# A hybrid encoder trunk on one core: a Fourier front whose roots, folds and first squares stand elsewhere

## The chip, the cores and the metric

The kernel runs on one core of a Trainium2 chip. The metric is the device time of one execution in microseconds (us); several executions are timed and their median is given.

## The reference

Two sequences of 512 tokens with 1024 channels, a prompt and a sample, go through two layers. The first mixes tokens by a grouped two-dimensional Fourier transform, the second by attention; each is followed by a squared-ReLU MLP. All arithmetic is float32. The change lies in the first mixer:

```python
def rms_norm(x, g):
    y = x32 * lax.rsqrt(jnp.mean(x32 * x32, axis=-1, keepdims=True) + EPS)
    return (y * g)

def fourier_mix(h, w_out):
    hg = h.reshape(B, S, N_FGROUPS, F_GROUP)          # 8 groups of 128 channels
    f = jnp.fft.fft2(hg, axes=(1, 3), norm="ortho").real
    return f.reshape(B, S, D_MODEL) @ w_out

for i in range(DEPTH):                                # DEPTH = 2
    if i % 2 == 0:
        x = x + fourier_mix(rms_norm(x, fourier_norm[j]), fourier_w_out[j])
    else:
        x = x + gqa_attention(rms_norm(x, attn_norm[j]), ...)
    x = x + sq_relu_mlp(rms_norm(x, mlp_norm[i]), mlp_w_up[i], mlp_w_down[i])
return rms_norm(x, final_norm)
```

## The kernel before

The engines are called by the names of the profile: PE does matrix products, DVE is the vector engine, ACT the scalar engine, POOL is GpSimd, and SP issues most DMAs. A float32 product is made of three products of halves: a value is split into a high half (a rounding copy by ACT, L86) and a low half (the difference, by DVE, L87). Everything that the change touches stands in one block in which the instructions of every engine run in the order in which the code was written; after some 90 us the rest of the two layers follows.

The first 75 us or so of that block, with `q=0` for the prompt and `q=1` for the sample:

- **Front.** `f0` and `f1` each take two of the prompt's four tiles of 128 tokens (`g0` and `g1` those of the sample). `squares` (L430) sums the squares of a tile's rows on ACT, `chain` makes the root of the mean from it (the five steps of `log_steps`: one of ACT's, with a logarithm and an exponential, L141 and L142, and four short ones of DVE, L145 to L149, for both tiles at once), `gain` multiplies by the norm's gain, `plus` and `minus` add and subtract the two halves of 512 channels, `scale` (L461), `scale_both` (L467) and `combine` multiply by the root. While the first inputs land, PE runs filler products (`idle`, L603).
- **The exact transform** (`transform(0)`). Along the tokens, the prompt's transform runs in plain float32, in three parts `k=0, 1, 2` (f0's two tiles, then f1's pair). Each part has, for each block `j` of 128 channels, an even product of 258 columns (`exact_even`, L531) and an odd one of 256 (`exact_odd`, L534), and a small one for the last frequency (`exact_nyq`, L537). Three blocks are accumulated over `k=0, 1`, each even and odd product in a PSUM bank of its own; after `mid()` come the `k=2` products, and the fourth block follows with all its six products after the first feature stage. `seq_evac` copies a block out, `feat_stage` transforms it along the channels (L571, L579, L580), and its result is split into halves `uv`.
- **The weights' folds.** `Fold(j)` holds two 128x1024 parts of `w_four`: DVE subtracts them (L672), and a DMA issued by POOL adds the second part from memory to the first (L673). `odd` splits the difference, `even_hi` and `even_lo` (L682, L686) the sum. `FoldNyq` does the same for the last frequency: three small operations of POOL (L701 to L703), a DMA to memory, and three DMAs back (L706).
- **Products with the folds.** `odd_outs` (L81 to L83) makes eight outputs, `k` outermost, from the halves `uv` and the odd folds; `even_outs` makes them one output at a time from the even folds, with a last product for the last frequency (L724).
- **The sample's transform** (`transform(1)`) runs in halves. Its `hook1` places the prompt's first MLP squares (`square`, L167, ACT) between the copies that PE waits for; POOL adds up the eight squares (L173), the sum is split (L195, L199), and PE's root product (L213) needs it.

Of the kernel before, what the change touches and what calls it, by code (L numbers as in the profile page):

```python
# [19 lines left out]
P = 128  # L20
D = 1024
# [23 lines left out]
def trunk_kernel(ctx, tc, x_in, xt_in, y_out, tables, rope, gfour, gcol, grow, gfin,  # L45
# [375 lines left out]
    class Front:  # L421


        def __init__(self, q, c):
            self.q, self.c = q, c
            self.ss, self.r = small(2), small(2)
            self.steps = log_steps(self.r[:, :2], self.ss[:, :2], 2, 1.0 / D)
            self.xg, self.p, self.m = [None] * 2, [None] * 2, [None] * 2

        def squares(self, i):  # L430
            sumsq(xa[self.q, 2 * self.c + i], self.ss[:, i : i + 1])
# [19 lines left out]

        def chain(self, a, b):
            for step in self.steps[a:b]:
                step()
            if b == 5 and self.c == 0 and self.q:
                self.rm = small(1)
                nc.gpsimd.tensor_mul(self.rm[:, :1], self.r[:, 1:2], mask)
# [12 lines left out]
        def combine(self):  # L470
# [9 lines left out]
            n = sm.tile([P, 2, 64], F32R, tag="ny", name=nm("ny"), bufs=2)  # L480
            nc.gpsimd.memset(f32(n), 0.0)
# [48 lines left out]
    def exact_even(k, j, o):  # L530
        nc.tensor.matmul(o[:, :258], parts[k][0][:, j * P : (j + 1) * P], cosX[k], start=k == 0, stop=k == 2)  # L531

    def exact_odd(k, j, v):
        nc.tensor.matmul(v[:, :256], parts[k][1][:, j * P : (j + 1) * P], sinX[k], start=k == 0, stop=k == 2)  # L534
# [16 lines left out]
    def seq_evac(q, o, v):  # L551
        if q == 0:
            t = slot([P, 514], F32)
            nc.scalar.copy(t[:, :258], o[:, :258])
            nc.scalar.copy(t[:, 258:], v[:, :256])
            return t[:, :258], t[:, 258:]
# [12 lines left out]
    def feat_stage(q, j, a, b, an, en, u=None):  # L569
        if q == 0:  # L570
            nc.tensor.matmul(u[:, :258], ftX[:, :P], a, start=False, stop=True)  # L571
# [6 lines left out]
        if q == 0:  # L578
            nc.tensor.matmul(v[:, :256], ftX[:, P:], b, start=True, stop=True)  # L579
            nc.tensor.matmul(en[0:72, :258], pickX[:, pick], a, start=j == 0, stop=j == 3)  # L580
# [10 lines left out]
    def nyq_out(q, en):  # L591
        t = slot([P, 258], F32R)[0:72]
        nc.scalar.copy(t, en[0:72, :258])
        nc.vector.tensor_sub(t[64:72], en[64:72, :258], f32(t[64:72]))
        un[q] = t
# [9 lines left out]
    def transform(q, mid=lambda: None, hook=lambda at, j: None):  # L605
        on, ov = ps(), [(ps(), ps()) for _ in range(3)]
        if q == 0:
            for k in range(2):
                for j in range(3):
                    exact_even(k, j, ov[j][0])  # L610
                exact_nyq(k, on)
                for j in range(3):
                    exact_odd(k, j, ov[j][1])
            mid()
            exact_nyq(2, on)
        else:
            seq_nyq(q, 0, on)
# [1561 lines left out]
```

## Time and profile before

| what | value |
|---|---|
| median of 3 executions | 1665.58 us (1665.34 to 1665.73) |
| profiled execution, its own time | 1665.18 us |
| span of that execution | 1663.4 us, so 1.78 us lie around the span |
| busy, of the span | DVE 1267.9 us (76%), ACT 882.2 (53%), POOL 383.7 (23%) |
| granted TensorE clock | 9 tenths or more of full speed in each of 40 slices |

The span runs from the first to the last instruction that the profiler recorded. Times in the timeline views are counted from its start.

### The profile page before, as it was taken

How to read it: one execution, taken by the hardware profiler on the slowest of the kernel's cores; microseconds unless marked ns; L12 is line 12 of the kernel's file. 1: busy time of each engine (PE TensorE's matmuls, PEld its weight loads, DVE VectorE, ACT ScalarE, POOL GpSimd, SP SyncE). 2: the span in 40 equal slices, each digit the busy share in tenths (PEclk: the TensorE clock that was granted, in tenths of full speed). 3: DMA queues.
4: the chain of work that ended last, by engine and by line, in shares of the span. 5: the costliest groups of instructions: out<-in, count | busy, mean ns of one | idle time of the engine just before them, and what ended most of it. 6: DMA issues, size and time to landing. Idle time of an engine off the chain costs nothing.

```text
span 1663.4 us, 22119 instructions
## 1 busy us (share of the span) xinstructions
PE 1653.9 (99%) x7768; PEld 1380.1 (83%) x7768; DVE 1267.9 (76%) x1818; ACT 882.2 (53%) x1566; POOL 383.7 (23%) x363
## 2 busy tenths in 40 slices
PE   9999999999999999999999999999999999999998
PEld 8988888888888888888888888888888888888887
DVE  8898786557886869868788878877855487878875
ACT  7776454446343425447688856554554553433335
POOL 3311443222000001324544303004422220000002
PEclk9999999999999999999999999999999999999999
DMA  9843554359775757425401146334544696757532
GB/s 310 255 159 133 191 209 171 140 186 373 239 234 167 242 181 231 171 72 196 171 1 39 64 172 231 129 108 178 202 147 169 222 375 194 232 161 231 180 108 102
DMA packets 122336, 302.48 MB, mean 182 GB/s; under 512 B 12360, under 2 KB 13768, under 8 KB 122224
## 3 DMA queue, kind: packets, MB, share of 16 engines
q1 hardware_dynamic: 98864, 253.66, 43.4%
q0 software_dynamic: 8960, 21.05, 5.9%
q10 hardware_dynamic: 14400, 26.35, 4.2%
q8 instruction: 61, 1.00, 0.2%
q14 instruction: 51, 0.42, 0.1%
HBM read 217.59 MB, written 82.38 MB: 180 GB/s over the span
## 4 chain that ended last, share of the span: by engine, by line
PE 98%; DVE 1%; issue 0%; DMA 0%; ACT 0%; POOL 0%; POOLq 0%; DVEq 0%; SPq 0%
PE ps L983 76%; PE ps L83 6%; PE ps L81 6%; PE ps L82 6%; PE ps L1586 2%; PE ps L1565 0%; DMA u<-x 0%; DVE u L437 0%; PE ps L213 0%; PE ps L534 0%; PE ps L531 0%; DVE u L1928 0%; POOL t L1580 0%; DVE t L450 0%; DVE t L441 0%
## 5 line engine op out<-in xcount | busy, mean ns | idle before, releaser
L983 PE MATMUL ps<-u,w 128*128 128x512 f32 x4944 | 1129.9, 389 | 0.0
L983 PEld LDWEIGHTS ps<-u,w 128*128 128x128 f32 x4944 | 927.1, 188 | 195.1 <-ACT u L1018 2.4
L86 ACT CAST w<-raw 128x1024 fp32r<-128x1024 f32 (+1 forms) x216 | 213.4, 994 | 312.3 <-PE ps L983 232.4
L87 DVE TENSOR_TENSOR w<-raw,w 128x1024 fp32r<-128x1024 f32 (+1 forms) x216 | 250.5, 1164 | 63.4 <-ACT w L86 59.5
L86 ACT CAST u<-u 128x1024 fp32r<-128x1024 f32 x144 | 144.8, 1048 | 87.6 <-PE ps L983 35.2
L87 DVE TENSOR_TENSOR u<-u,u 128x1024 fp32r<-128x1024 f32 x144 | 173.0, 1229 | 20.8 <-ACT u L86 20.2
L983 PE MATMUL ps<-u,u 128*128 128x512 f32 x600 | 142.8, 389 | 0.0
L1202 DVE TENSOR_TENSOR u<-ps,u 128x512 f32<-128x512 f32 x160 | 109.4, 685 | 39.7 <-PE ps L983 37.0
L1103 POOL TENSOR_TENSOR u<-u 128x512 f32<-128x512 f32 x28 | 37.8, 1352 | 428.8 <-ACT u L1000 428.8
L1229 POOL DMA_DIRECT2D raw<-w_sum x32 | 27.7, 865 | 468.3 <-DVE w L87 165.4
L983 PEld LDWEIGHTS ps<-u,u 128*128 128x128 f32 x600 | 112.6, 188 | 23.4
L81 PE MATMUL ps<-u,u 128*128 128x512 f32 (+2 forms) x340 | 128.6, 380 | 0.0
L83 PE MATMUL ps<-u,u 128*128 128x512 f32 (+2 forms) x340 | 123.7, 365 | 0.0
L82 PE MATMUL ps<-u,u 128*128 128x512 f32 (+2 forms) x340 | 123.6, 364 | 0.0
L173 POOL TENSOR_TENSOR t<-t,t 128x512 f32<-128x512 f32 (+1 forms) x49 | 69.3, 1419 | 185.7 <-ACT t L167 184.9
L999 ACT ACTIVATE t<-t 128x512 f32<-128x512 f32 x64 | 40.4, 631 | 111.1 <-DVE t L1072 101.3
L83 PEld LDWEIGHTS ps<-u,u 128*128 128x128 f32 x340 | 64.2, 189 | 10.4 <-DVE u L87 0.3
L87 DVE TENSOR_TENSOR u<-ps,u 128x512 fp32r<-128x512 f32 (+3 forms) x112 | 68.0, 634 | 6.1 <-ACT u L86 5.7
L82 PEld LDWEIGHTS ps<-u,u 128*128 128x128 f32 x340 | 64.4, 189 | 8.5 <-DVE u L87 0.8
L81 PEld LDWEIGHTS ps<-u,u 128*128 128x128 f32 x340 | 64.4, 189 | 7.7
L1059 DVE TENSOR_TENSOR t<-ps,u 128x512 f32<-128x512 f32 x32 | 22.0, 688 | 62.0 <-PE ps L983 51.4
L86 ACT CAST u<-ps 128x512 fp32r<-128x512 f32 (+3 forms) x112 | 59.0, 555 | 7.5 <-PE ps L1586 5.8
(269 smaller groups left out, 2016.3 us busy)
## 6 DMA issues: line engine op xcount, KB each, us to landing
raw<-w_up SPq DMA_DIRECT2D x80, 512.0 KB, 4.5
u<-spill_t SPq DMA_DIRECT2D x60, 512.0 KB, 7.0
raw<-w_sum SPq DMA_DIRECT2D x56, 512.0 KB, 5.4
u<-spill_b SPq DMA_DIRECT2D x45, 512.0 KB, 6.1
spill_t<-u SPq DMA_DIRECT2D x84, 256.0 KB, 2.0
spill_b<-t ACTq DMA_DIRECT2D x60, 256.0 KB, 4.1
raw<-w_row SPq DMA_DIRECT2D x28, 512.0 KB, 4.6
park<-u SPq DMA_DIRECT2D x24, 512.0 KB, 4.3
```

Source lines behind the costliest of these rows:

```text
L81: nc.tensor.matmul(out, lh, rh, start=first, stop=False)
L82: nc.tensor.matmul(out, lh, rl, start=False, stop=False)
L83: nc.tensor.matmul(out, ll, rh, start=False, stop=last)
L86: hi = nc.scalar.copy(dst_hi, src)
L87: return hi, eng.tensor_sub(dst_lo, src, f32(dst_hi))
L173: nc.gpsimd.tensor_add(acc[q][:, :n], acc[q][:, :n], s[:, :n])
L983: nc.tensor.matmul(o, w[x][:, sl], h[k][y], start=first and k + i == 0, stop=k == n - 1 and i == 2, skip_group_check=not first)
L999: nc.scalar.activation(t, src, AF.Relu)
L1103: eng.tensor_sub(t[:, 0], b12, b11)
L1202: return nc.vector.tensor_add(x, o, x)
L1229: nc.gpsimd.dma_start(s[:, 1], w[:, 3], accum_op=ALU.add)
L1586: nc.tensor.transpose(pt[:, t * P : (t + 1) * P], probs[t][:, sc * P : (sc + 1) * P], ident)
```

## The change

- A root is made by POOL, tile by tile, with two operations on 128x1 values (`root`: add eps, raise to the power -1/2), in place of `chain`; ACT's square is scaled so that it sums the mean. There are 22 fillers instead of the second run of 26.
- In the exact transform, the even product (now 257 columns) and the odd one (255) of a block share a PSUM bank, so that four banks hold four blocks: the fourth block's `k=0, 1` products are done with the others. One copy of 128x512 takes a block out.
- For folds 2 and 3, DVE writes the difference to a new buffer and POOL adds on chip (`tensor_add`, 128x1024), instead of the adding DMA. `FoldNyq`'s small operations come after f1's second root, and its DMAs back (`spread`) after fold 1's `minus`. The even halves of folds 2 and 3 are made ahead of those of 0 and 1.
- The first two even outputs are made together, `k` outermost.
- In `transform(1)`, the squares that stood after the first three blocks (`seq`) stand after the third block, the first feature stage, the fourth block, the second stage, and two each after the third and fourth stages.

```diff
         def __init__(self, q, c):
-            self.steps = log_steps(self.r[:, :2], self.ss[:, :2], 2, 1.0 / D)
         def squares(self, i):
-            sumsq(xa[self.q, 2 * self.c + i], self.ss[:, i : i + 1])
+            if self.q and i == 0:
+                self.n = sm.tile([P, 2, 64], F32R, tag="ny", name=nm("ny"), bufs=2)
+                nc.gpsimd.memset(f32(self.n), 0.0)
+            junk = tm((P, 1024), BF16)
+            nc.scalar.activation(junk, xa[self.q, 2 * self.c + i], AF.Square, scale=D ** -0.5,
+                                 accum_out=self.ss[:, i : i + 1])
+        def root(self, i):
+            nc.gpsimd.tensor_tensor(out=self.ss[:, i : i + 1], in0=self.ss[:, i : i + 1], in1=eps, op=ALU.add)
+            nc.gpsimd.tensor_tensor(out=self.r[:, i : i + 1], in0=self.ss[:, i : i + 1], in1=half, op=ALU.pow)
+            if i and self.c == 0 and self.q:
+                self.rm = small(1)
+                nc.gpsimd.tensor_mul(self.rm[:, :1], self.r[:, 1:2], mask)
         def gain(self, i, k=None, o=None):
...
-        def chain(self, a, b):
-            for step in self.steps[a:b]:
-                step()
-            if b == 5 and self.c == 0 and self.q:
-                self.rm = small(1)
-                nc.gpsimd.tensor_mul(self.rm[:, :1], self.r[:, 1:2], mask)
...
     def exact_even(k, j, o):
-        nc.tensor.matmul(o[:, :258], parts[k][0][:, j * P : (j + 1) * P], cosX[k], start=k == 0, stop=k == 2)
-    def exact_odd(k, j, v):
-        nc.tensor.matmul(v[:, :256], parts[k][1][:, j * P : (j + 1) * P], sinX[k], start=k == 0, stop=k == 2)
+        nc.tensor.matmul(o[:, :257], parts[k][0][:, j * P : (j + 1) * P], cosX[k][:, :257], start=k == 0, stop=k == 2)
+    def exact_odd(k, j, o):
+        nc.tensor.matmul(o[:, 257:], parts[k][1][:, j * P : (j + 1) * P], sinX[k][:, 1:], start=False, stop=k == 2,
+                         skip_group_check=True)
     def exact_nyq(k, o):
...
     def seq_evac(q, o, v):
         if q == 0:
-            t = slot([P, 514], F32)
-            nc.scalar.copy(t[:, :258], o[:, :258])
-            nc.scalar.copy(t[:, 258:], v[:, :256])
-            return t[:, :258], t[:, 258:]
+            t = slot([P, 512], F32)
+            nc.scalar.copy(t, o)
+            return t[:, :257], t[:, 257:]
...
     def transform(q, mid=lambda: None, hook=lambda at, j: None):
-        on, ov = ps(), [(ps(), ps()) for _ in range(3)]
+        on = ps()
         if q == 0:
+            ov = [(ps(), None) for _ in range(NT)]
-                for j in range(3):
+                for j in range(NT):
-                for j in range(3):
-                    exact_odd(k, j, ov[j][1])
+                for j in range(NT):
+                    exact_odd(k, j, ov[j][0])
             mid()
+            ov = [(ps(), ps()) for _ in range(3)]
...
-        o3 = ps(), ps()
+        o3 = (ps(), ps()) if q else ov[3]
         if q == 0:
-            for k in range(3):
-                exact_even(k, 3, o3[0])
-            for k in range(3):
-                exact_odd(k, 3, o3[1])
+            exact_odd(2, 3, o3[0])
+            exact_even(2, 3, o3[0])
...
         def minus(self):
-            nc.vector.tensor_sub(self.b, self.a, self.b)
-            nc.gpsimd.dma_start(self.a, w_four[1, self.j], accum_op=ALU.add)
+            if self.j < 2:
+                nc.vector.tensor_sub(self.b, self.a, self.b)
+                nc.gpsimd.dma_start(self.a, w_four[1, self.j], accum_op=ALU.add)
+                return
+            b, self.b = self.b, slot([P, D], F32)
+            nc.vector.tensor_sub(self.b, self.a, b)
+            nc.gpsimd.tensor_add(self.a, self.a, b)
         def odd(self):
...
         def load(self):
+        def fold(self):
+        def spread(self):
...
         wn.load()
-        idle(ps(), 26)
-        f0.squares(0)
-        f0.squares(1)
+        idle(ps(), 22)
+        for i in range(2):
+            f0.squares(i)
+            f0.root(i)
-        f0.chain(1, 2)
+        f0.plus(0)
+        f0.minus(0)
+        f0.scale_both(0)
+        for k in range(2):
+            f0.gain(1, k, halves_gr[k])
+        f0.plus(1)
+        f0.minus(1)
-        f0.minus(0)
-        f0.chain(0, 1)
-        f0.chain(2, 5)
-        f0.plus(0)
-        f0.scale_both(0)
-        f0.gain(1)
-        f0.minus(1)
-        f0.plus(1)
+        f1.root(0)
+        f1.minus(0)
+        f1.plus(0)
-        f1.chain(1, 2)
-        f1.minus(0)
+        f1.root(1)
+        wn.fold()
+        f1.scale()
+        f1.minus(1)
+        f1.plus(1)
         fold = [Fold(j) for j in range(2)]
         def mid():
-            f1.chain(0, 1)
-            f1.plus(0)
-            f1.chain(2, 5)
-            f1.scale()
-            f1.minus(1)
-            f1.plus(1)
...
             if at == "seq":
                 if j == 0:
+                    wn.spread()
                 elif j == 2:
...
             elif j == 3:
-                g0.squares(0)
-                g0.gain(0)
-                g0.minus(0)
-                g0.plus_there(0)
-                g0.squares(1)
-                g0.gain(1)
-                g0.minus(1)
-                g0.plus_there(1)
+                for i in range(2):
+                    g0.squares(i)
+                    g0.root(i)
+                for i in range(2):
+                    fold[2 + i].even_hi()
+                    g0.gain(i)
+                    g0.minus(i)
+                    g0.plus_there(i)
         transform(0, mid, hook0)
-        g0.chain(0, 2)
+        for i in range(2):
+            fold[2 + i].even_lo()
+        g0.scale(slice(0, 1))
+        fold[0].even_lo()
-        g0.chain(2, 5)
-        fold[0].even_lo()
-        g0.scale(slice(0, 1))
-        fold[2].even_hi()
-        fold[2].even_lo()
-        odd_put(0, 0, o[0])
-        fold[3].even_hi()
-        fold[3].even_lo()
-        for fo in range(1, 4):
+        for fo in range(2):
+            odd_put(0, fo, o[fo])
+        for fo in range(2, 4):
...
-        def even(fo):
-            even_put(0, fo, even_outs(0, [fo])[0])
+        def even(fo, o=None):
+            even_put(0, fo, o or even_outs(0, [fo])[0])
         g1.squares(0)
-        even(0)
+        g1.root(0)
+        o = even_outs(0, range(2))
+        even(0, o[0])
         g1.squares(1)
-        even(1)
+        g1.root(1)
+        even(1, o[1])
-        g1.chain(0, 2)
-        g1.chain(2, 5)
...
+        due = iter(range(KC))
         def hook1(at, j):
-            if at == "seq":
-                if j < 3:
-                    square(0, j)
-            else:
-                square(0, 3 + j)
-                if j == 3:
-                    square(0, 7)
+            for _ in range({("seq", 2): 1, ("feat", 0): 1, ("seq", 3): 1, ("feat", 1): 1,
+                            ("feat", 2): 2, ("feat", 3): 2}.get((at, j), 0)):
+                square(0, next(due))
         transform(1, hook=hook1)
```

PE's rows of the exact transform up to the first feature stage (L531 and L534, now L534 and L537, are the even and odd products, the 40-row ones those of the last frequency; the bank stands ahead of the arrow). Before, from the first products of `k=1` on:

```order
L531 MATMUL ps_261<-u_110,t_223 128x258
L537 MATMUL ps_256<-u_110,ny_213 40x258
L534 MATMUL ps_258<-u_116,t_221 128x256
L534 MATMUL ps_260<-u_116,t_221 128x256
L534 MATMUL ps_262<-u_116,t_221 128x256
L537 MATMUL ps_256<-u_116,ny_289 40x258
L534 MATMUL ps_258<-u_116,t_285 128x256
L531 MATMUL ps_257<-u_116,t_278 128x258
```

And of the change:

```order
L534 MATMUL ps_250<-u_110,t_199 128x257
L541 MATMUL ps_246<-u_110,ny_192 40x258
L537 MATMUL ps_247<-u_116,t_201 128x255
L537 MATMUL ps_248<-u_116,t_201 128x255
L537 MATMUL ps_249<-u_116,t_201 128x255
L537 MATMUL ps_250<-u_116,t_201 128x255
L541 MATMUL ps_246<-u_116,ny_269 40x258
L537 MATMUL ps_247<-u_116,t_230 128x255
L534 MATMUL ps_247<-u_116,t_216 128x257
```

Each part now has a fourth block's product (bank ps_250) ahead of the products that wait for f1 (t_230, t_216; before t_285, t_278); four such products come there from the place after the first feature stage.

POOL's rows from its first arithmetic on. Before:

```order
L701 TENSOR_TENSOR u_158<-u_158 128x64
L702 CAST u_158<-u_158 128x64
L703 TENSOR_TENSOR u_158<-u_158 128x64
L704 DMA nyq<-u_158 128x2x64
L706 DMA u_155<-nyq 8x1024 x3
L673 DMA raw_238<-w_four 128x1024
L673 DMA raw_242<-w_four 128x1024
L673 DMA raw_297<-w_four 128x1024
L673 DMA u_301<-w_four 128x1024
```

And of the change, from f1's second root on:

```order
L439 TENSOR_TENSOR s_148<-s_147,half 128x1
L713 TENSOR_TENSOR u_152<-u_152 128x64
L714 CAST u_152<-u_152 128x64
L715 TENSOR_TENSOR u_152<-u_152 128x64
L716 DMA nyq<-u_152 128x2x64
L679 DMA raw_234<-w_four 128x1024
L679 DMA raw_238<-w_four 128x1024
L720 DMA u_149<-nyq 8x1024 x3
L683 TENSOR_TENSOR raw_277<-raw_277,u_278 128x1024
L683 TENSOR_TENSOR u_281<-u_281,u_282 128x1024
```

Four roots (eight rows) stand ahead of `FoldNyq` now, and the two adds of folds 2 and 3 (L683) are queued behind the three DMAs that wait for `nyq`.

ACT's rows in `transform(1)` (L86 copies the halves that PE waits for, L167 are the squares). Before, from the first square on:

```order
L167 ACTIVATE t_832<-u_427 128x512
L86 CAST u_842<-ps_785 128x258
L86 CAST t_843<-ps_786 128x256
L167 ACTIVATE t_848<-u_427 128x512
L86 CAST u_859<-ps_787 128x258
L86 CAST t_860<-ps_788 128x256
L167 ACTIVATE t_865<-u_428 128x512
L86 CAST u_879<-ps_868 128x257
L86 CAST u_879<-ps_873 128x255
L167 ACTIVATE t_884<-u_428 128x512
```

And of the change, the same copies from the second block on:

```order
L86 CAST u_812<-ps_757 128x258
L86 CAST t_813<-ps_758 128x256
L86 CAST u_826<-ps_759 128x258
L86 CAST t_827<-ps_760 128x256
L167 ACTIVATE t_832<-u_415 128x512
L86 CAST u_845<-ps_834 128x257
L86 CAST u_845<-ps_839 128x255
L167 ACTIVATE t_850<-u_415 128x512
```

The first square stands where the third stood, and the second where the fourth stood.

## Rows read from the trace of the kernel before

**Rows 1.** The page: busy time, share of the span and instructions of PE.

```profile
PE 1653.9 (99%) x7768; PEld 1380.1 (83%) x7768; DVE 1267.9 (76%) x1818; ACT 882.2 (53%) x1566; POOL 383.7 (23%) x363
```

**Rows 2.** PE's waits: line, releaser, then total us, times, longest.

```profile
PE ps L537 <- DVE ny L475: 0.4, 1, 0.4
PE ps L531 <- ACT t L467: 0.4, 1, 0.4
...
PE ps L1586 <- POOL t L1580: 0.2, 1, 0.2
```

**Rows 3.** Timeline of PE, 5 to 30 us: start, us, engine, line.

```profile
5.92 3.56 PE L603 MATMUL ps<-u 128*128 128x256 f32 x26
9.84 1.57 PE L531 MATMUL ps<-u,t 128*128 128x258 f32 x6 [0.36 <-ACT t L467]
...
15.26 1.56 PE L534 MATMUL ps<-u,t 128*128 128x256 f32 x6
17.25 0.63 PE L537 MATMUL ps<-u,ny 128*40 128x258 f32 x2 [0.44 <-DVE ny L475]
...
20.55 0.60 PE L531 MATMUL ps<-u,t 128*128 128x258 f32 x2
...
29.64 0.28 PE L81 MATMUL ps<-u,u 128*128 128x256 f32 x1
```

**Rows 4.** Timeline of ACT, 4 to 21 us.

```profile
5.80 0.19 ACT L130 ACTIVATION_READ_ACCUMULATOR t<-u 128x1 f32 x1
...
9.06 0.72 ACT L467 ACTIVATE t<-t,s 128x512 f32<-128x512 f32 x1 [0.26 <-DVE t L441]
...
14.30 0.19 ACT L130 ACTIVATION_READ_ACCUMULATOR t<-u 128x1 f32 x1
```

**Rows 5.** Timeline of DVE, 4 to 42 us.

```profile
6.31 0.69 DVE L437 TENSOR_TENSOR u<-u,ps 128x512 f32<-128x512 f32 x1 [0.17 <-PE ps L382]
...
18.57 1.22 DVE L672 TENSOR_TENSOR u<-raw,u 128x1024 f32<-128x1024 f32 x1
...
26.74 1.22 DVE L87 TENSOR_TENSOR u<-u,u 128x1024 fp32r<-128x1024 f32 x1
27.87 2.07 DVE L87 TENSOR_TENSOR u<-ps,u 128x257 fp32r<-128x257 f32 x6
```

**Rows 6.** Timeline of POOL, 3 to 58 us.

```profile
12.01 0.79 POOL L701 TENSOR_TENSOR u<-u 128x64 f32<-128x64 f32 x1 [9.55 <-DMA u<-w_nyq]
...
13.53 1.18 POOL L703 TENSOR_TENSOR u<-u 128x64 fp32r<-128x64 f32 x1
...
20.84 1.55 POOL L706 DMA_DIRECT2D u<-nyq  x3 [4.85 <-DMA nyq<-u]
```

**Rows 7.** One line of POOL, last in the kernel: duration ns min/median/max, starts.

```profile
L1910 POOL TENSOR_TENSOR s<-s,half x2: 667/812/957, 1654.8 to 1658.6; 128x1 f32<-128x1 f32 x2
```

**Rows 8.** Timeline of POOL and of DVE at 88 us: both read two tiles.

```profile
88.65 1.30 POOL L173 TENSOR_TENSOR t<-t,t 128x512 f32<-128x512 f32 x1 [19.18 <-ACT t L167]
...
89.26 1.78 DVE L278 TENSOR_TENSOR u<-u,u 128x1024 fp32r<-128x1024 f32 x1
```

**Rows 9.** Timelines of ACT, POOL, DVE and PE, 56 to 73 us.

```profile
60.94 0.69 ACT L167 ACTIVATE t<-u 128x512 f32<-128x512 f32 x1
...
59.58 4.03 POOL L173 TENSOR_TENSOR t<-t,t 128x512 f32<-128x512 f32 x3 [1.13 <-ACT t L167]
64.06 5.41 POOL L173 TENSOR_TENSOR t<-t,t 128x512 f32<-128x512 f32 x4 [0.45 <-ACT t L167]
...
70.16 0.69 DVE L199 TENSOR_TENSOR u<-t,u 128x512 fp32r<-128x512 f32 x1 [0.23 <-ACT u L195]
...
71.45 0.63 PE L213 MATMUL ps<-u,minus 128*128 128x512 f32 x2
```

**Rows 10.** Timelines of DVE and PE at 56 us.

```profile
56.12 0.68 DVE L506 TENSOR_TENSOR u<-t,u 128x512 fp32r<-128x512 f32 x1
...
56.85 0.28 PE L83 MATMUL ps<-u,u 128*128 128x258 f32 x1
```

More of the change, by code (lines that the diff above doesn't have):

```diff
@@ L479, in combine @@
                 return
-            n = sm.tile([P, 2, 64], F32R, tag="ny", name=nm("ny"), bufs=2)
-            nc.gpsimd.memset(f32(n), 0.0)
+            n = self.n
             n32 = sm.tile([P, 16], F32, tag="n32", name=nm("n32"), bufs=2)
@@ L570, in feat_stage @@
         if q == 0:
-            nc.tensor.matmul(u[:, :258], ftX[:, :P], a, start=False, stop=True)
+            nc.tensor.matmul(u[:, :257], ftX[:, :P], a, start=False, stop=True)
         else:
@@ L578, in feat_stage @@
         if q == 0:
-            nc.tensor.matmul(v[:, :256], ftX[:, P:], b, start=True, stop=True)
-            nc.tensor.matmul(en[0:72, :258], pickX[:, pick], a, start=j == 0, stop=j == 3)
+            nc.tensor.matmul(v[:, 1:256], ftX[:, P:], b, start=True, stop=True)
+            nc.tensor.matmul(en[0:72, :257], pickX[:, pick], a, start=j == 0, stop=j == 3)
         else:
@@ L591, in nyq_out @@
     def nyq_out(q, en):
-        t = slot([P, 258], F32R)[0:72]
-        nc.scalar.copy(t, en[0:72, :258])
-        nc.vector.tensor_sub(t[64:72], en[64:72, :258], f32(t[64:72]))
+        t, n = slot([P, 258], F32R)[0:72], 258 if q else 257
+        if q == 0:
+            nc.gpsimd.memset(f32(t[:, 257:]), 0.0)
+        nc.scalar.copy(t[:, :n], en[0:72, :n])
+        nc.vector.tensor_sub(t[64:72, :n], en[64:72, :n], f32(t[64:72, :n]))
         un[q] = t
@@ L627, in transform @@
             if q == 0:
-                exact_odd(2, j, ov[j][1])
+                exact_odd(2, j, ov[j][0])
                 exact_even(2, j, ov[j][0])
```

## The prediction

> **What bounds the kernel now.** The page comes first: PE is busy for 1653.9 of 1663.4 us [rows 1], so only PE's idle time, and work taken off PE, can change the time. Second the list of what PE waits for: two of 0.4 us lie in the exact transform, and the only one after the first 80 us is of 0.2, on L1586 [rows 2]. What the change does in those 80 us is therefore handed on unchanged to the end, if no later margin catches it. Third the timelines of the front, engine by engine. The reader should see in PE's that fillers run from 5.92 us, the first exact product starts at 9.84, the products of `k=0, 1` end at about 16.66 (a row of six instructions starts at 15.26 and shows 1.56 us, of which the last 0.17 is the modelled tail), the small product of f1 starts at 17.25, and the last of its row group at 20.55 [rows 3]. Each exact product is two instructions, about 0.433 us.
>
> 0.2% of the time is 3.3 us; that is what a measurement of this kernel can tell from no change.
>
> **The change, part by part.**
>
> *Start of the exact transform: -1.0 us.* The first product waited for ACT's scale of 0.72 us at 9.06, which waited for the root and DVE [rows 4]. Now the square of tile 0 is read out at 5.99 us [rows 4], and the root needs two POOL operations. A power on 128x1 takes 0.67 to 0.96 us [rows 7]; the add I take at 0.5 (below 0.79, which POOL needs for 64 columns [rows 6]). So the root is there at 7.2 to 7.5. DVE's second gain starts at 6.31 and ends at 7.0 [rows 5], the `plus` behind it needs as much, to 7.7, and the scale 0.72, to 8.4. PE's fillers end at 9.48 in the row, of which some 0.16 is modelled tail, so that a product could have followed at 9.32; 26 in 3.56 us are 0.12 to 0.13 each, and four fewer end at 8.84. PE goes on there without a wait: 9.84 - 8.84 = 1.0 us. If both operations took 1.18 us, POOL's longest small one [rows 6], the root came at 8.35, the scale ended at 9.07, and 0.8 were left.
>
> *The fourth block's first products ahead: -0.9 us.* From 16.66 to the end of the last exact product at 20.55 + 0.43 = 20.98 pass 4.3 us [rows 3]. Its work is one small product (0.43 and 0.13 for switching) and six of 0.43, with 0.1 for switching: 3.3. The missing 1.0 us is PE waiting for f1's `combine`. Four products of 0.43 (1.7 us) now stand ahead of it, so PE comes to f1's part at 8.84 + 6.8 + 1.7 = 17.4, when the first result of `combine`, for which the row at 17.25 waited, should be there and the other two follow before their products. I take 0.9 off. The four products are moved, not saved; the columns saved (258 to 257, 256 to 255, 18 products and the feature stage) are about 0.06 us. One ACT copy for two is hidden behind PE, which runs other blocks meanwhile. So far -2.0 us: the odd outputs would start their second one, at 29.64 before [rows 3], at 27.6.
>
> *POOL adds folds 2 and 3 on chip: +2.4 us.* An add of 128x512 takes 1.30 us on POOL [rows 8]; one of 128x1024 so about 2.6. The trace shows what it does to DVE: at 88.65 POOL starts such an add, which ends at 89.95; DVE starts a subtraction of two tiles at 89.26, and needs 1.78 us for it, though other subtractions of that size take 1.22 [rows 5, 8]. 1.78 is the 0.69 until POOL is done and 1.09 of its own: DVE waited for all of POOL's instruction. POOL in turn needed 1.18 us for 64 columns at 13.53 [rows 6]. The Trainium skill says this outright ("SBUF — State Buffer", Who interferes with whom): a DVE instruction with two SBUF inputs and a GpSimd instruction that reads SBUF hold the pair of ports that they share for a whole instruction, whoever comes first. The rule agrees with the two rows, and speaks against giving POOL long adds here; the next sentences need only the rows.
>
> When do the adds run? They are queued behind `spread`, which waits for the landing of `nyq`. Before, from the start of POOL's first small operation at 12.01 to the end of the three DMA issues at 20.84 + 1.55 = 22.39 pass 10.4 us [rows 6]. Now that sequence starts after f1's second root: the square is read out at 14.49 [rows 4], two operations of 0.5 and 0.7 later it is 15.7, and the first add may start at 26.1. DVE goes through the same rows from 18.57 on, about 0.35 us earlier, since four short operations are gone; its split of fold 2, at 26.74 [rows 5], would start at 26.4. So POOL is first by a hair, DVE's split waits until 28.7 and ends at 29.9. Behind it in DVE's queue are the six low halves of `uv` (27.87 before, [rows 5]), which free the banks that the second and later odd outputs use. Each frees one bank in 0.34 us, each output takes 0.36: PE waits once, from 27.5 to 29.9, that is 2.4 us. Bounds: 0, if the lock were none or the order lucky; 1.2, if both engines shared evenly; 2.6. If DVE is first, its low halves (one input in PSUM) run beside POOL, and the second add instead holds up the low halves of the even folds that follow; that costs between 0 and 2.6 at the even outputs. I take 2.4, because the row at 89.26 is of the same two kinds.
>
> The two adding DMAs that go away free memory traffic, which nothing here waits for.
>
> *Squares later, first two even outputs together: +0.9 us.* POOL's first add started at 59.58, right behind the second square. This square now takes the place of the fourth, which ended at 60.94 + 0.69 = 61.63 beside the same PE work [rows 9]. So the first add starts at 61.7. Seven adds take 4.03 + 5.41 = 9.44 us without a pause (before, 0.45 of pause lay between), to 71.15 instead of 69.47. From there to the end of DVE's low half at 70.85 before are 1.4 us; so it comes at 72.5, and PE's root product stood at 71.45 [rows 9]: 1.05 late. ACT is less loaded early, so I take 0.9. The two squares in a row also delay the last feature stage's copies; a wait there would only take part of the same 0.9 earlier. The pairing of even outputs changes no PE work; it gives the even folds' low halves more time.
>
> *Sum:* -1.0 - 0.9 - 0.06 + 2.4 + 0.9 = +1.3 us. The profiled execution took 1665.18, so 1666.5; the median lies 0.4 above it: **1666.9 us**, no change that could be measured.
>
> **The rivals.**
>
> *No lock on the path (faster, within 0.2%).* POOL's adds run beside DVE rows with PSUM inputs, or the order falls luckily. For it: of DVE's rows at 27.87, six have a PSUM input; against it: 26.1 and 26.4 are close, and both adds must fall well. -2.0 + 0.9 = -1.1: 1664.5. If the squares' margin held too: 1663.6. Even that is 2.0 below, less than 3.3.
>
> *The roots come late for the sample (slower).* Place: PE's row of the sample's transform at 56.85, whose operand DVE finishes at 56.80 [rows 10]. The margin is nothing, so each microsecond by which g1's root comes later than PE's own shift is paid in full. Its price: a small POOL operation took 1.18 us beside DVE's long ones [rows 6] instead of 0.5 to 0.7; four of them in g0's chain and four in g1's, at +0.5 each, make up to 4 us, of which about 1.3 is already in PE's shift. That adds up to 3: 1669.9. It decides when add and power together take over 1.3 us. For it speaks that g0's and g1's roots run while DVE does splits of two inputs; against it that eight short DVE operations of the old chain, one ACT logarithm and one exponential are gone from the same paths.
>
> *The change does nothing there:* if DMA landings rather than the roots set the start (tile 0's input), the 1.0 is not had: +2.3, 1667.9.
>
> **How the numbers follow.** Forecast +1.3 (between 0 and +3.3): 0.5. No lock cost: 0.25. Late roots: 0.2. No gain at the start: 0.05. The range from 1664.4 to 1670.0 takes in the no-lock case and late roots; outside are the ideal case and mishaps together. Slower by over 3.3 us: the greater part of the late roots, 0.19. Faster by over 3.3: nothing above adds up to it, 0.03. Within 0.2%: 0.78.
>
> **What would show it.** Right: the first exact product near 8.8; no wait at f1's small product; one wait of about 2.4 us on a low half (L87) in the odd outputs, with a POOL add of some 2.6 us in front of that DVE row; a wait on L199 or so at the root product of up to 0.9. Wrong: POOL's adds starting after the odd outputs' banks are free, DVE rows of normal length beside them, a wait in the sample's transform (late roots), or a root that takes 2 us at the start.

## The result, and the profile after

The change takes 1668.59 us in the median of 22 executions (1666.52 to 1669.63), the kernel before 1665.97 (1665.33 to 1667.09, also 22). The ratio is 1.0013, 95% interval 1.0007 to 1.0019: about 2.2 us slower (the two medians lie 2.6 apart). That is within 0.2%, inside the range and on the forecast's side of zero, but 1.7 us above the predicted time; and the interval lies wholly above 1, so the difference can be measured, which the forecast denied. The profiled execution took 1667.65 us.

The page shows that PE's work is the same, so the time was lost in waits; a longer span holds 1654.1 us of it [rows 1]:

```profile
PE 1654.1 (99%) x7764; PEld 1379.4 (83%) x7764; DVE 1266.7 (76%) x1803; ACT 880.6 (53%) x1554; POOL 397.9 (24%) x380
```

PE's waits (line, releaser, total, times, longest). The two of the exact transform [rows 2] are gone; three others have come, on a low half in the odd outputs, late in the kernel (L993), and at the sum's root (L213):

```profile
PE ps L81 <- DVE u L87: 2.1, 1, 2.1
...
PE ps L993 <- DVE t L1212: 0.4, 1, 0.4
...
PE ps L213 <- DVE u L199: 0.2, 1, 0.2
```

PE's timeline shows the gain and its end. The first exact product starts at 8.29 us (9.84 in [rows 3]), the small product of f1 follows without a wait at 16.91, and the second odd output, which would have come at 27.1, comes at 29.37 (29.64 before):

```profile
8.29 2.00 PE L534 MATMUL ps<-u,t 128*128 128x257 f32 x8
...
15.00 1.99 PE L537 MATMUL ps<-u,t 128*128 128x255 f32 x8
16.91 0.63 PE L541 MATMUL ps<-u,ny 128*40 128x258 f32 x2
...
26.96 0.28 PE L83 MATMUL ps<-u,u 128*128 128x256 f32 x1
29.37 0.39 PE L81 MATMUL ps<-u,u 128*128 128x256 f32 x1 [2.14 <-DVE u L87]
```

What held it is seen by laying DVE's timeline beside POOL's. First DVE, then POOL, of the change:

```profile
24.41 3.44 DVE L682 TENSOR_TENSOR u<-u,u 128x1024 f32<-128x1024 f32 x1
27.77 1.21 DVE L87 TENSOR_TENSOR u<-u,u 128x1024 fp32r<-128x1024 f32 x1
28.91 2.06 DVE L87 TENSOR_TENSOR u<-ps,u 128x257 fp32r<-128x257 f32 x6
```

```profile
22.82 1.56 POOL L720 DMA_DIRECT2D u<-nyq  x3 [1.51 <-DMA nyq<-u]
24.39 2.36 POOL L683 TENSOR_TENSOR raw<-raw,u 128x1024 f32<-128x1024 f32 x1
27.93 3.31 POOL L683 TENSOR_TENSOR u<-u,u 128x1024 f32<-128x1024 f32 x1 [1.18 <-DVE u L682]
```

DVE's subtraction of fold 3 takes 3.44 us instead of 1.22: it starts 0.02 us behind POOL's add, and lasts until 1.10 us after that add's end at 26.75. The three other traces with these adds (old place of squares, second trace, wait filled) bear this out: DVE's row starts 0.19, 0.32 and 0.57 us behind POOL's add there and takes 3.28, 3.15 and 2.90 us, and each time it ends 1.10 us after the add. The low halves that free PE's banks are queued behind it and start at 28.91 (27.87 in [rows 5]). POOL's second add in turn waits for DVE's split at 27.77.

The squares' place shows in PE's rows of the sample's outputs: a gap ahead of L82 at 66.70, which needs the last low half, and one ahead of the second half of the root product, which waits for DVE's low half L199 (both halves ran from 71.45 on in [rows 9]):

```profile
66.03 0.28 PE L83 MATMUL ps<-u,w 128*128 128x258 f32 x1
66.19 0.39 PE L81 MATMUL ps<-u,w 128*128 128x258 f32 x1
66.70 0.39 PE L82 MATMUL ps<-u,w 128*128 128x258 f32 x1
...
72.65 0.50 PE L213 MATMUL ps<-u,minus 128*128 128x512 f32 x1 [0.17 <-DVE u L199]
```

To follow the loss through the kernel, PE's rows of two traces are laid side by side, counted back from the last (from the odd outputs on their order is the same). The table gives how much later a row starts than in the trace of the kernel before, at the time given for that trace; negative is earlier. That trace, of an execution of 1665.18 us, is one of the fastest of its kernel. A trace is of one execution, whose own time is given, and that can lie some way from the median. One execution of the kernel with folds by DMA took 7922.44 us, everything in it almost five times as long; it is left out of the median, and the row is that of a second trace.

| trace of | 28 us | 35 | 64 | 89.8 (MLP starts) | 1500 | 1656 | traced execution, us | median us (executions) |
|---|---|---|---|---|---|---|---|---|
| the change | -2.55 | -0.17 | -0.14 | +1.08 | +1.15 | +2.11 | 1667.65 | 1668.59 (22) |
| the change, second trace | -1.87 | +1.71 | +1.74 | +2.97 | +2.93 | +2.93 | 1668.47 | 1668.47 (1) |
| folds by DMA | -1.91 | -1.74 | -0.64 | +0.59 | +0.91 | +0.91 | 1666.11 | 1665.62 (10) |
| old place of squares | -2.00 | +1.72 | +1.75 | +1.75 | +1.70 | +1.81 | 1667.31 | 1666.87 (11) |
| both | -2.19 | -2.03 | -0.35 | +0.67 | +0.69 | +2.08 | 1667.27 | 1665.82 (11) |
| POOL only writes | -1.70 | -1.54 | +4.82 | +6.07 | +6.10 | +6.14 | 1671.31 | 1671.31 (1) |
| change, wait filled | | +0.47 | +0.50 | +1.73 | +3.00 | +4.20 | 1669.74 | 1668.66 (11) |
| before, delayed | | +1.14 | +1.14 | +1.14 | +1.41 | +1.54 | 1666.71 | 1667.31 (11) |
| before, squares moved | +0.36 | +0.36 | +0.36 | +1.58 | +1.88 | +1.92 | 1667.12 | 1666.99 (11) |
| folds by DMA, squares between | -2.55 | -2.40 | -0.59 | +0.64 | +1.09 | +1.09 | 1666.27 | 1665.59 (11) |
| both, fourth block last | -0.84 | -0.86 | -0.72 | -0.63 | -0.56 | +0.17 | 1665.36 | 1665.36 (1) |
| both, roots as before | +2.36 | +2.57 | +3.73 | +3.73 | +4.18 | +4.17 | 1669.37 | 1669.37 (1) |

The change is 2.55 ahead, loses 2.4 at the odd outputs and 1.2 between 66 and 74 us, and starts the MLP 1.08 late: +1.3 was the forecast.

### The profile page after: what moved, and what is told of

Same layout as the page of the kernel before. It is cut to its first block, busy times and chain, and to the rows that moved or that the text cites. A ratio compares the mean times of both kernels' runs of the same rounds, so it can differ in the third digit from the quotient of the medians.

```text
span 1665.9 us, 22109 instructions
## 1 busy us (share of the span) xinstructions
PE 1654.1 (99%) x7764; PEld 1379.4 (83%) x7764; DVE 1266.7 (76%) x1803; ACT 880.6 (53%) x1554; POOL 397.9 (24%) x380
## 4 chain that ended last, share of the span: by engine, by line
PE 95%; DVE 2%; DMA 1%; issue 1%; ACT 1%; POOL 1%; POOLq 0%; DVEq 0%; ACTq 0%
PE ps L993 74%; PE ps L83 6%; PE ps L81 6%; PE ps L82 6%; PE ps L1596 2%; POOL t L173 0%; PE ps L1575 0%; DMA raw<-w_sum 0%; DVE u L87 0%; DMA u<-spill_t 0%; DVE u L1938 0%; DVE u L682 0%; PE ps L537 0%; ACT u L86 0%; PE ps L534 0%
## 5 line engine op out<-in xcount | busy, mean ns | idle before, releaser
L993 PE MATMUL ps<-u,w 128*128 128x512 f32 x4944 | 1130.1, 389 | 0.0
L993 PEld LDWEIGHTS ps<-u,w 128*128 128x128 f32 x4944 | 927.1, 188 | 195.4 <-ACT u L1028 2.4
L86 ACT CAST w<-raw 128x1024 fp32r<-128x1024 f32 (+1 forms) x216 | 213.3, 994 | 307.4 <-PE ps L993 230.8
L86 ACT CAST u<-u 128x1024 fp32r<-128x1024 f32 x144 | 144.8, 1047 | 91.7 <-PE ps L993 38.2
L993 PE MATMUL ps<-u,u 128*128 128x512 f32 x600 | 143.1, 389 | 0.4 <-DVE t L1212 0.4
L993 PEld LDWEIGHTS ps<-u,u 128*128 128x128 f32 x600 | 112.6, 188 | 24.2 <-DVE t L1212 0.8
L82 PE MATMUL ps<-u,u 128*128 128x512 f32 (+2 forms) x340 | 123.5, 364 | 0.0
L82 PEld LDWEIGHTS ps<-u,u 128*128 128x128 f32 x340 | 64.4, 189 | 8.6 <-DVE u L87 0.8
L86 ACT CAST u<-ps 128x512 fp32r<-128x512 f32 (+3 forms) x112 | 58.9, 554 | 7.9 <-PE ps L1596 5.8
```

The costliest lines, as they stand in the source:

```text
L82: nc.tensor.matmul(out, lh, rl, start=False, stop=False)
L86: hi = nc.scalar.copy(dst_hi, src)
L993: nc.tensor.matmul(o, w[x][:, sl], h[k][y], start=first and k + i == 0, stop=k == n - 1 and i == 2, skip_group_check=not first)
```

## Experiments

**Folds 2 and 3 by DMA.** The order that goes with it is restored too:

```diff
         def minus(self):
...
-            b, self.b = self.b, slot([P, D], F32)
-            nc.vector.tensor_sub(self.b, self.a, b)
-            nc.gpsimd.tensor_add(self.a, self.a, b)
+            nc.vector.tensor_sub(self.b, self.a, self.b)
+            nc.gpsimd.dma_start(self.a, w_four[1, self.j], accum_op=ALU.add)
...
-                    fold[2 + i].even_hi()
+                    fold[i].even_hi()
...
```

> The change, but folds 2 and 3 are added by the DMA as before, their even halves made after those of folds 0 and 1 again, and the first two outputs of the odd products put away ahead of fold 3's halves. Theory (POOL's adds hold DVE up): the wait of 2.1 us on a low half in the odd outputs is gone, DVE's subtraction of fold 3 takes 1.2 us instead of 3.4, and the first product of the MLP (90.9 us in the trace of the change, 89.8 before) stands at 89 to 89.5; the wait at the sum's root stays. Rival 1 (PE's head start is worth nothing since the even folds come no earlier): the wait reappears, 1 to 2 us, at the first even outputs, and the MLP starts at 90 to 91. Rival 2 (DVE's long row has another cause): the row of 3.4 us stays.

1665.62 us median, ratio to before 0.9997 (0.9988 to 1.0006). The kernel once more, for the trace that is read here:

> The first experiment's kernel once more, for a trace that is not disturbed: folds 2 and 3 by DMA, squares as in the change. By the theory of the lock no wait of PE in the odd outputs, the MLP's start at 89 to 89.9 us, and in time about 1665.6; by the rival a wait at the first even outputs of over 1 us.

1666.11 us. DVE's timeline in that trace, and PE's second odd output:

```profile
25.05 1.22 DVE L677 TENSOR_TENSOR u<-u,u 128x1024 f32<-128x1024 f32 x1
26.19 1.22 DVE L87 TENSOR_TENSOR u<-u,u 128x1024 fp32r<-128x1024 f32 x1
```

```profile
27.60 0.28 PE L83 MATMUL ps<-u,u 128*128 128x256 f32 x1
27.80 0.39 PE L81 MATMUL ps<-u,u 128*128 128x256 f32 x1
```

The long row and the wait are gone; PE is still 1.74 ahead at 35 us. By the MLP it is 0.59 late all the same, at 90.4 us and so later than expected: 0.5 go at the even outputs, 0.6 at the sample's transform, 1.2 at the squares. So the lock's theory holds for the odd outputs, and the first rival has half a point: PE's head start meets folds and inputs that come when they came before.

**POOL busy, but only writing.** Is it POOL's work as such, or the order restored above? Here folds 2 and 3 go by DMA in the change's order, with memsets of POOL behind each:

```diff
...
+            if self.j >= 2:
+                junk = slot([P, D], F32)
+                for _ in range(3):
+                    nc.gpsimd.memset(junk, 0.0)
```

> The change, folds 2 and 3 added by the DMA, but at the place of each of POOL's adds stand three memsets of 128x1024 that only write (nothing reads what they write). Theory of a lock between two-input reads: DVE's subtraction of fold 3 takes 1.2 us as alone and the wait in the odd outputs is gone, though POOL is as busy as with its adds. Rival (any POOL work there slows DVE, or POOL's queue is what is late): the row stays at 2 to 3.5 us. The even folds come late by the DMA here, so a wait at the first even outputs of 1 to 3 us is expected by both.

DVE and POOL in this trace:

```profile
25.26 1.21 DVE L677 TENSOR_TENSOR u<-u,u 128x1024 f32<-128x1024 f32 x1
26.39 1.22 DVE L87 TENSOR_TENSOR u<-u,u 128x1024 fp32r<-128x1024 f32 x1
```

```profile
25.33 3.36 POOL L682 MEMSET u<- 128x1024 f32 x3
```

POOL is busy from 25.33 to 28.69, and DVE's two rows in that time take what they take alone. The Trainium skill states just this ("SBUF — State Buffer", Who interferes with whom): only a GpSimd instruction that reads SBUF contends with DVE's two-input ones, not one that only writes. This trace agrees, with 1.21 us against 3.44. No wait comes in the odd outputs, so the order restored in the first experiment was not what removed it. The late even folds cost more than the 1 to 3 us expected: PE waits 4.4 us at the first even output (wait list), and behind that wait, from 45 to 48 us, the granted clock is 0.50. Between 35 and 64 us the trace loses 6.4 us in all, some 1.7 of it at the low clock.

```profile
PE ps L81 <- ACT u L761: 4.4, 1, 4.4
```

**Squares where they stood.** Here `hook1` is that of the kernel before.

> The change with the prompt's first squares where they stood before. Theory: the two late waits (0.75 us at the last product of the first even output, 0.45 at the sum's root) go away, and the MLP starts 1.1 us earlier than in the change, at about 89.7, as before; time 1 us below the change. Rival (the waits come from DVE or POOL being late for other reasons): they stay within 0.3 us.

1666.87 us, ratio 1.0004 (0.9995 to 1.0013). Between 64 and 89.8 us nothing is lost (+1.75 and +1.75): both late waits are gone. But the trace starts the MLP at +1.75, not at 0. It lost 1.5 us between 30 and 35 us, where PE waits for nothing. That was new, and is taken up below.

**Both.**

> Both: folds 2 and 3 by DMA in the order of the first experiment, and squares where they stood. Theory: what PE wins at the start (about 2 us) is kept as far as the even folds allow; the MLP starts at 88 to 88.8, 1 to 1.8 us before the kernel before, time 1664 to 1665. Rival (the even folds are the limit): it starts at 89.5 to 90, no gain over the kernel before.

1665.82 us, ratio 0.9999 (0.9990 to 1.0008); no gain, as the rival says, and the MLP starts later than even the rival had it, at 90.5 us (+0.67). PE, 2.0 us early at 35 us, loses 0.9 at the even outputs, as the rival has it, 0.4 by 60 us, and 1.4 from there to 67 us: the first square, now ahead of the copies that PE needs, had to wait for its input, which had not come, and what ACT has to do behind it came late. ACT's row:

```profile
58.80 0.63 ACT L167 ACTIVATE t<-u 128x512 f32<-128x512 f32 x1 [1.60 <-DMA u<-xt]
```

**The squares alone**, in the kernel before:

> The kernel before with only the squares moved as in the change. Theory of the prediction (the adds of POOL, 9.4 us from the second square on, are late for the sum's root): 0.8 to 1.05 us slower than before, as a wait at the last feature stage's low half (about 0.4 to 0.7) and one at the root product (the rest). Rival (only a wait for the input's landing, which the kernel before does not have, made the squares late): within 0.3 us of before.

1666.99 us, 1.0 above before (ratio 1.0006, 0.9997 to 1.0015: the interval takes in 1, so it is the trace that shows the loss). From 64 to 89.8 us the trace loses 1.22 us, 0.75 at the last low half and 0.47 at the root product. No landing is involved; the term stands by itself.

**Squares between**, one place earlier than in the change, with folds by DMA:

```diff
-            {("seq", 2): 1, ("feat", 0): 1, ("seq", 3): 1, ("feat", 1): 1, ("feat", 2): 2, ("feat", 3): 2}
+            {("seq", 1): 1, ("seq", 2): 1, ("feat", 0): 1, ("seq", 3): 1, ("feat", 1): 1, ("feat", 2): 1, ("feat", 3): 2}
```

> Folds 2 and 3 by DMA as in the first experiment, and each of the first six squares one place earlier than in the change (the first behind the second block, so still behind the landing of its input). Theory: POOL's adds start about 1 us earlier, the waits at the last feature stage's low half (0.7) and at the root product (0.45) go away, and the MLP starts 1.1 to 1.3 us earlier than in the first experiment's trace, about 0.6 us before the kernel before; time 1664.5 to 1665.3. Rival: ACT, not the squares' place, is full there, and the 0.7 stays.

1665.59 us, ratio 0.9998 (0.9989 to 1.0007). The wait at the root product is gone, but the loss at the last low half grows from 0.75 to 1.23 us, so that nothing is won: from 64 us to the MLP this trace loses 1.23 (-0.59 to +0.64), and the first experiment's as much (-0.64 to +0.59). The MLP starts 0.64 behind the kernel before, where 0.6 ahead was expected; the rival is right. Again the first square waits for its input, and ACT has hardly a pause behind it:

```profile
59.00 0.63 ACT L167 ACTIVATE t<-u 128x512 f32<-128x512 f32 x1 [0.73 <-DMA u<-xt]
```

**The fourth block last**, and **the roots as before**, each in the kernel with both parts undone:

```diff
-                for j in range(NT):
+                for j in range(3):
                     exact_even(k, j, ov[j][0])
...
```

> The kernel with both parts undone (folds by DMA, squares as before), and the fourth block's products of the first two parts put back behind the first feature stage. Theory: the wait for f1 comes back (0.6 to 0.9 us at the small product and the first odd one), and PE reaches the odd outputs that much later (25 to 27 us in those traces). Rival: the roots alone made f1 early enough, and nothing changes.

PE's timeline shows the two waits on f1 again:

```profile
16.39 0.63 PE L541 MATMUL ps<-u,ny 128*40 128x258 f32 x2 [0.16 <-DVE ny L479]
17.17 0.70 PE L537 MATMUL ps<-u,t 128*128 128x255 f32 x2 [0.16 <-DVE t L480]
```

From the first exact product (9.36) to the first odd output (28.24) pass 18.88 us, with the fourth block ahead 18.13 (8.76 to 26.89): 0.75, as expected. Yet this trace starts the MLP 1.3 us before that of the kernel it is made from: hardly any of the later waits up to the MLP appears. Its 1665.36 us, of one execution, is below every median here, though single executions of other kernels are shorter (1664.99 of the kernel with both parts undone).

```diff
         def root(self, i):
-            nc.gpsimd.tensor_tensor(out=self.ss[:, i : i + 1], in0=self.ss[:, i : i + 1], in1=eps, op=ALU.add)
-            nc.gpsimd.tensor_tensor(out=self.r[:, i : i + 1], in0=self.ss[:, i : i + 1], in1=half, op=ALU.pow)
+            if i == 0:
+                return
+            for step in log_steps(self.r[:, :2], self.ss[:, :2], 2, 1.0):
+                step()
```

> The kernel with both parts undone, with the roots made as before, for both tiles at once by one logarithm and exponential of ACT and four short operations of DVE. Theory: the first exact product waits for the root of both tiles and starts 0.8 to 1.8 us later, and a wait of up to 1 us at f1's small product appears. Rival: the fillers, not the root, set the start, and it stays within 0.3 us.

More than expected. PE's first product, and the granted clock by windows (first PE's busy time, then PEld, DVE, ACT, POOL, the clock, DMA):

```profile
11.53 3.68 PE L536 MATMUL ps<-u,t 128*128 128x257 f32 x8 [3.14 <-ACT t L473]
```

```profile
8.00:11.50 3.50, 0.40 (x4) 0.19 (x2) 3.16 (x8) 0.94 (x3) 0.00 (x0) 1.00 1.04 407
11.50:13.00 1.50, 1.47 (x4) 1.19 (x5) 1.47 (x3) 1.47 (x4) 0.57 (x2) 0.52 1.01 400
13.00:14.00 1.00, 1.00 (x4) 0.82 (x3) 1.00 (x3) 1.00 (x2) 0.92 (x2) 0.50 1.02 406
```

The root of both tiles, in this order of the work, makes PE wait for 3.14 us where the other traces of this front have no wait, and then its first eight products take 3.68 us instead of 2.00, at half the clock (1.2 GHz). No wait at f1's product appears; PE comes too late for it.

**The change once more, for its two groups of times.** Its 22 executions fall apart: ten lie at 1666.52 to 1667.65 us, twelve at 1668.48 to 1669.63, none between. The profiled one was of the lower group.

> The change once more, for a second trace. If this execution falls into the upper group of its times (above 1668.4 us), the theory of the clock expects the granted clock at its lower level for about 3 us behind the wait of 2.1 us in the odd outputs, worth 1.6 to 1.8 us; a rival expects that time at the waits near 1515 us. If it falls into the lower group, no stretch of lower clock.

1668.47 us, upper group. The granted clock behind the wait:

```profile
26.00:29.00 3.00, 1.91 (x11) 1.43 (x9) 3.00 (x2) 2.09 (x5) 1.82 (x2) 1.00 1.06 279
29.00:30.00 1.00, 0.23 (x2) 0.23 (x3) 1.00 (x4) 1.00 (x2) 1.00 (x1) 1.00 1.11 283
30.00:31.00 1.00, 1.00 (x9) 1.00 (x9) 1.00 (x5) 1.00 (x3) 1.00 (x1) 0.80 0.94 262
31.00:32.00 1.00, 1.00 (x6) 1.00 (x6) 0.94 (x4) 1.00 (x3) 0.96 (x4) 0.50 1.02 284
32.00:33.00 1.00, 1.00 (x7) 1.00 (x6) 1.00 (x2) 1.00 (x2) 0.96 (x1) 0.50 0.40 98
33.00:34.00 1.00, 1.00 (x7) 1.00 (x7) 1.00 (x2) 1.00 (x2) 1.00 (x2) 0.50 0.08 27
34.00:36.00 2.00, 2.00 (x18) 2.00 (x18) 1.97 (x3) 1.21 (x3) 1.84 (x3) 1.00 0.00 1
```

PE waits 1.9 us, starts again at full clock, falls to 0.50 for some three microseconds, with 6 to 7 products in one instead of about 9, and is 1.5 later for it (+0.23 at 30 us to +1.71 at 35, in the table's terms). No wait near 1515 us appears in this trace. The trace with the squares' old place shows the same stretch; that is its unexplained 1.5.

Two traces do not make a rule for 22 executions, but the mean granted clock of each execution is on record too, to three places, and a stretch like this one is worth 0.001 of it. Of the upper group's twelve executions ten have 0.998 or 0.997; of the lower group's ten nine have 0.999. Every recorded execution of the kernel before has 0.999 or 1.000. In the kernel with the squares' old place the four executions with 0.998 lie at 1667.31 to 1667.76 us, and six of the seven with 0.999 at 1665.28 to 1666.87. So the clock goes with the groups, though not in each execution.

**The wait filled with work.**

```diff
         o = [ps()[:, :n] for _ in fos]
+        if q == 0 and extra is None:
+            idle(o[0], 17)
```

> The change with 17 filler products (0.12 us each, 2.0 us) put into the first odd output's bank ahead of its first real product, so that PE works during most of the time in which it waits for DVE's low half. Theory (the executions of the change above 1668.4 us are those in which PE's clock falls to its lower level after the 2.1 us of idleness): all executions lie at 1666.5 to 1667.7, the median 1.5 to 2 us below the change, the granted clock shows no lower stretch, and the MLP starts at most 0.3 us later than in the change's trace. Rival (they have another cause, such as the wait near 1515 us): half of the executions still lie above 1668.4. Rival 2 (fillers simply delay PE): 2 us slower than the change.

1668.66 us (1666.69 to 1670.39), ratio 1.0014 (1.0005 to 1.0023). The trace has no stretch of lower clock, and starts the MLP 1.24 us before the second trace of the change; but the times did not come together, and the median did not fall: six of eleven executions lie above 1668.4, as the first rival has it. Nine of the eleven, four of those six among them, have a mean clock of 0.999, so here it is hardly the clock that makes them long. (The traced one has 0.998 without such a stretch, so a single figure proves little.) This trace loses another 2.5 us late, 1.3 of it between 1000 and 1300 us and 1.2 between 1500 and 1535. So my theory of one cause for all the spread fell.

**A bare delay** in the kernel before, the same line with 9 fillers:

> The kernel before with 9 filler products (1.1 us) ahead of its first odd output: PE is late by as much as the change is at the start of the MLP, with nothing else changed. Theory (a shift at the front is handed on unchanged): 1.1 us slower than before, in all executions within 1 us of each other. Rival (the wait near 1515 us, 0.7 to 1.3 us in the traces of the change and of the kernel with both parts undone, comes from the shift): 2 us slower, with that wait in the trace.

1667.31 us, 1.3 above before (ratio 1.0008, 0.9999 to 1.0017); its trace goes from +1.14 at the MLP to +1.54. The shift is handed on nearly unchanged, and it does not bring the wait near 1515 us in this trace. The executions do not lie within 1 us of each other, as expected, but within 2.6 (1666.32 to 1668.89).

## Why the prediction came out as it did

*Start, -1.0:* the size is right in the mean, and the 1.55 of the first trace is in part luck. In the nine traces of this front with the new roots PE's first product follows its fillers without a wait, as predicted, at 8.29 to 9.39 us; in the kernel before and its two variants it waits for ACT's scale and comes at 9.84, 9.88 and 10.20. The means, 8.94 and 9.97, differ by 1.0. The sum had no term for the spread. It goes with the fillers' speed: 22 of them take 2.87 us in the two traces that start at 8.29 and 8.30, and 3.41 in the one that starts at 9.39, and between 5 and 6 us PE has 11 or 12 products in those two and 6 to 8 in the other seven. The first twelve fillers of every trace take 2.93 us, so PE begins at about half its later speed, and when that ends differs between executions; the profile's clock figure, 1.00 there, does not show it. The root of tile 0 took 0.19 and 0.56 us, less than assumed, but did not set the start.

*Fourth block ahead, -0.96 with the columns:* from the first product to the first odd output 18.24 us instead of 19.25, 1.01. Right, and 0.75 of it by the block alone.

*POOL's adds, +2.4:* the mechanism was right, and the size too, 2.3 us between 27.1 and 29.37; the row was not. (The working also let PE go on at the end of DVE's split; in the trace PE starts 0.46 us after the first low half behind it does, 28.91 to 29.37.) `FoldNyq`'s operations took 0.40, 0.24 and 0.66 us instead of the 0.79, 0.58 and 1.18 of [rows 6], and began 0.4 earlier than assumed, so the add came at 24.39, not 26.1. DVE came to its rows 1.2 us earlier than before, not 0.35, and the add met the subtraction of fold 3 instead of the split of fold 2. That POOL was first was no luck of one execution: it was so in all four traces.

*Squares, +0.9:* 1.2 in both traces of the change and, alone, in the kernel before.

*Sum, +1.3:* the first trace has +1.08 at the MLP, and the second would have some +1.5 without its stretch of low clock (2.97 less 1.5). What is missing is behind it. The step that failed is that the wait costs only its length: twelve of 22 executions, the median among them, lie 2.0 us higher in the mean than the others (1669.0 against 1667.0), and the one trace of that group shows the lower clock and 1.5 us lost. That the clock makes the two groups is borne out by the clocks on record, but was not shown by an experiment: with the wait filled the stretch was gone and the median was not lower. That the lower group lies close to the predicted 1666.9 is luck in part: its trace has both an early start and a late loss that the sum did not have. The line "handed on unchanged to the end" failed with that loss: the first trace loses 1.0 between 1500 and 1535 us, where DVE waits 2.2 us for a DMA that adds to a weight (wait list of that stretch):

```profile
DVE raw L1280 <- DMA raw<-w_sum: 3.5, 2, 2.2
```

In all twelve traces of the table the loss there goes with that wait: the four in which the longest is 2.0 to 2.2 us lose 0.7 to 1.4 us, the eight in which it is 0.8 to 1.6 lose 0.1 at most.

*The rivals:* no lock, excluded by the trace. Late roots, excluded at the sample's transform for the change (-0.14 before and behind it). The gain at the start not had: excluded.

*What stays open:* why that DMA lands late in some executions and not in others, and what else is lost late (1.3 us between 1000 and 1300 us with the wait filled); the kernel before has a spread too, its executions reach from 1665.14 to 1667.89. Why the first trace of the change, with the longest wait of the three (2.14 against 1.9 and 2.0), kept its clock. And why the kernel with the fourth block last starts the MLP earlier than that with the block ahead: both are 0.7 ahead at 58 us, and the 1.3 arise behind it, where the input of the first square is there in time in the one and not in the other; what set that input's place in the queue was not followed.

No version tried is measurably faster than the kernel before: the three medians below it (1665.59 to 1665.82) have intervals that take in 1. The traces show where the head start ends. With folds by DMA PE comes to 35 us 1.7, 2.0 and 2.4 us ahead; at 48 us, behind the even outputs, it is 1.1 to 1.2 ahead in all three, and at 58 us, in the sample's transform, 0.6 to 0.7. What PE has beyond that is lost there.

## What to carry to other kernels

Before giving POOL an add with operands in SBUF, lay its expected time beside DVE's rows with two SBUF inputs: each such pair runs one after the other, and what waits is all that DVE has queued behind, even where each engine has time to spare. A head start of PE is worth only as much as the latest of what it needs next: here it ran into folds, inputs and squares that kept their old times. A wait of about 2 us cost nearly twice its length in two traces, where the clock fell behind it (1.5 us on top of 1.9 and 2.0).

## What the hardware showed that was not expected

- Behind waits of 1.9, 2.0 and 4.4 us PE's granted clock fell to 0.50 some 0.6 to 0.8 us after work had resumed, and came back after about 3 us; behind one of 2.14 it did not. Behind one of 3.14 it was down at once.
- POOL's power on a 128x1 value took 0.55 to 0.57 us where DVE was free or read PSUM, and 0.89 to 1.48 beside DVE's two-input rows: a tiny operation can wait for most of the other engine's instruction.
- An add of 128x1024 on POOL took 2.36 us, less than twice that of 128x512 (1.30, [rows 8]).
